# Normed feed-forward inputs, down products in groups of four, and an even split of the PSUM banks in a two-block transformer kernel

## The chip, the cores and the metric

The kernel runs on one core of a Trainium2 chip. The metric is the time of one execution on the device in microseconds (us): the median of the runs shown, and for the trace one execution that was profiled. PE is the matrix engine, DVE the vector engine, ACT the scalar engine, POOL the GpSimd engine, SP the engine that issues most transfers. SBUF holds the tiles (128 partitions), PSUM takes the results of the matrix engine in 8 banks of 512 fp32 columns.

## The reference

L = 1040 tokens (16 meta tokens and 1024 of the input), model width 1024, all in fp32. Two layers, then a second block:

```python
for layer in range(2):
    h = rms_norm(hs, norm_mix_pre[layer])
    mix = pool_mixer(h, ...) if layer == 0 else sliding_window_attention(h, k_blk, v_blk, ...)
    hs = hs + rms_norm(mix, norm_mix_post[layer])
    h = rms_norm(hs, norm_ffn_pre[layer])
    hs = hs + rms_norm(swiglu(h, w_gate_up[layer], w_down[layer]), norm_ffn_post[layer])
    if layer == 0:
        kv_in = rms_norm(hs, kv_norm)      # k, v of the attention of layer 1
x = hs[:, 16:]
h = x * (1 + scale) + shift                # scale, shift, gate from silu(c) @ w_ada
p = h @ w_in
out_a = gmlp_branch(p[..., :1536])         # u * (causal spatial product of LN(v)) * silu(gate)
out_b = rwkv7_branch(p[..., 1536:])        # token shift, decay, scan over time, LN, gate
x = layer_norm(ALPHA * x + gate * (concat(out_a, out_b) @ w_out), ln_g, ln_b)
```

The feed-forward width is 2816, 22 blocks of 128 (`NF`). A root-mean-square norm is a per-token factor times a per-channel gain, so it can be applied to the input of a product or to its result.

## The kernel before, in words

Activations lie with channels on partitions: 8 tiles (`KT`) of 128 channels by up to 512 or 528 tokens. The tokens go in two halves, A and B. In layer 0 half A is two chunks of 264 tokens and half B one of 512; in layer 1 each half is one chunk of 512. All large products are done as three reduced-precision fp32 products, high by high, low by high and high by low (`mm3`), for which each input is split into a high part (an ACT copy, `xh`, `hh`, `wh`) and a low part (a DVE subtraction, `xl`, `hl`, `wl`). Weights are loaded 512 KB at a time by SP into `wr` and split by `split_weight` (ACT L329, DVE L330); four split sets and two raw ones are in the pool.

The program is written by generator threads that a planner (`run`, L220) steps: it takes the ready thread of highest priority, and a thread may yield planned time, wait for an event, or acquire a resource. That sets the order of the matrix engine's instructions. The other engines' instructions are ordered by priorities that `soon` raises. `main` (priority 0) runs `mixer0`, then four feed-forward passes a0A, a0B (layer 0), a1A, a1B (layer 1), then the second block of half B; `attentions` (priority 1) runs beside a0B and a1A and then does the second block of half A beside a1B; `out_first`, the output product of half A with its layer norm `final`, is spawned at priority -1 (L1619).

A feed-forward pass (`ffn`): for each f of 22, `up(f)` makes the gate product `pg` and the up product `pu` (8 x 3 matmuls each). Their inputs are the unnormed activations times the gain g, so the evictions multiply by the token factor `sb` of the norm: DVE L599 (gate times sb), ACT L604 (tanh of half of it), DVE L605, DVE L606 (up times sb), DVE L607 (the product `fg`), ACT L610 (`hh`), DVE L611 (`hl`). In a0A it is L599, a Silu, L602, L607. After two f's, `down` makes for each of 8 row blocks one PSUM tile of 2 x 3 matmuls and adds it to `acc` in SBUF (DVE L627; the first group copies, ACT L625). The last two f's go through `last` (L644), which makes the parts of three row blocks that don't need f = 21 first, finishes chunk by chunk and starts `finish` for each. `finish` (L394) norms the result, adds the old residual (L424, L425), stores it, splits hn x g into xh and xl (L435, L439), sets the event `x` on which the next pass starts, and only then works out the factor (`st_n`, `sb_n`; event `s`, waited for once per pass at f = 0).

`mixer0` does half A of the first mixer and spawns `second_half` (L535), which after the first finish reads blocks 5 to 9 in one burst (`blocks(5, 10)`) and makes the bands two at a time. In `second` (L1377), once half A is through, `rwkv(p, h)` for p = 0 to 3 acquires 15 tiles (`T`) each; `out_first` acquires 28 and gives 12 of them back when its `final` is done. At the start of half B two lines raise all priorities to their absolute value, so `out_first` runs then at +1. PSUM: pool `psg` (products) has 3 banks, `pss` (attention scores, rwkv and small products) 5.

Of the kernel before, what the change touches and what calls it, by code (L numbers as in the profile page):

```python
# [183 lines left out]
class K:  # L184
# [124 lines left out]
    def split_weight(self, src, name, gain=None, halves=False):  # L309
# [12 lines left out]
        ld = nc.sync.dma_start(out=raw, in_=src)  # L322
# [71 lines left out]
    def finish(self, y, sq, ch, ci, g_post, g_pre, src, dst, X):  # L394
# [21 lines left out]
        mod = g_pre == "mod"  # L416
        sqn = None if mod else self.ht(f"sqn_{nm}")
        for k in range(KT):
            fetch(k + 3)
            hn = y[k][:, s]  # L420
            if X["h"][k] is None:
                X["h"][k], X["l"][k] = self.ht(f"xh_{nm}_{k}", F32R), self.ht(f"xl_{nm}_{k}", F32R)
            xh, xl = X["h"][k][:, s], X["l"][k][:, s]
# [3 lines left out]
            if mod:  # L427
                t = self.tt(f"md_{nm}_{k}")[:, :w]
                nc.scalar.activation(out=t, in_=hn, func=AF.Identity, scale=self.mod[:, 8 + k:9 + k], bias=self.mod[:, k:k + 1])
                nc.scalar.activation(out=xh, in_=t, func=AF.Copy)  # L430
                nc.vector.tensor_tensor(out=xl, in0=t, in1=xh.bitcast(F32), op=ALU.subtract)
            else:
                g = None if g_pre is None else self.v(g_pre, k)
                self.sq_add(sqn, hn, w, k == 0, self.eng(X["name"], 2, k))
                nc.scalar.activation(out=xh, in_=hn, func=AF.Copy, **({} if g is None else dict(scale=g)))  # L435
                if g is None:
                    nc.vector.tensor_tensor(out=xl, in0=hn, in1=xh.bitcast(F32), op=ALU.subtract)
# [5 lines left out]
        if not mod:  # L443
            yield w_nsum
            dg = self.stats_sum(sqn, ch, f"n{nm}")
            yield w_nspread
            X["s"][ci] = self.stats_spread(dg, ch, f"n{nm}")
# [3 lines left out]
    def mixer0(self, Xs):  # L451
# [83 lines left out]
        def second_half():  # L535
# [3 lines left out]
            blocks(5, 10)  # L539
            yield 15000  # L540
            ch, y, sq = H0[1][0], [], self.ht("sqy0_10")
            for i in range(2):
                sp = [band(ch, "10", 2 * i + k) for k in range(2)]
                yield 9000
# [23 lines left out]
    def ffn(self, layer, X, chunks, tail):  # L568
# [6 lines left out]
        def up(f):  # L575
# [12 lines left out]
            for ci, (c0, w, _) in enumerate(chunks):  # L588
# [4 lines left out]
                if f == 0:  # L593
                    yield ("ev", f"s{nm}_{ci}")
                sb = X["s"][ci][:, :w]
# [1074 lines left out]
```

## Time and profile before

| | us |
|---|---|
| median of 3 runs (2833.78 to 2845.5) | 2837.9 |
| the profiled execution | 2839.37 |
| its span on the core | 2837.6 |

| engine | busy, share of the span |
|---|---|
| PE | 2629.9 us, 93% |
| DVE | 1745.2 us, 62% |
| ACT | 1068.7 us, 38% |
| POOL | 348.2 us, 12% |

The mean granted clock of the matrix engine is 0.956 of full speed. A share of busy time is an average: a stage in which PE is busy throughout at full clock can only be shortened by less work, one in which it waits or runs at a lower clock by an earlier arrival of what it waits for.

### The profile page before, as it was taken

How to read it: one execution, taken by the hardware profiler on the slowest of the kernel's cores; microseconds unless marked ns; L12 is line 12 of the kernel's file. 1: busy time of each engine (PE TensorE's matmuls, PEld its weight loads, DVE VectorE, ACT ScalarE, POOL GpSimd, SP SyncE). 2: the span in 40 equal slices, each digit the busy share in tenths (PEclk: the TensorE clock that was granted, in tenths of full speed). 3: DMA queues.
4: the chain of work that ended last, by engine and by line, in shares of the span. 5: the costliest groups of instructions: out<-in, count | busy, mean ns of one | idle time of the engine just before them, and what ended most of it. 6: DMA issues, size and time to landing. Idle time of an engine off the chain costs nothing.

```text
span 2837.6 us, 41913 instructions
## 1 busy us (share of the span) xinstructions
PE 2629.9 (93%) x16381; PEld 2183.1 (77%) x16381; DVE 1745.2 (62%) x3366; ACT 1068.7 (38%) x1996; POOL 348.2 (12%) x324
## 2 busy tenths in 40 slices
PE   5878999989999999999999999999999999999966
PEld 4868999978877877787778777877777777777756
DVE  6446665575666476756664774527756557666744
ACT  5333222354444333545443344323322224443423
POOL 3111000120000021100000210001101002311213
PEclk8888999999999999999999999999998999999968
DMA  4264433333222243332223444433232225443322
GB/s 151 98 143 135 153 123 97 96 123 101 90 64 82 89 141 101 130 100 79 88 69 101 141 134 133 127 129 116 73 110 63 97 90 196 153 137 118 104 94 67
DMA packets 156885, 314.57 MB, mean 111 GB/s; under 512 B 44792, under 2 KB 68778, under 8 KB 156688
## 3 DMA queue, kind: packets, MB, share of 16 engines
q1 hardware_dynamic: 147792, 296.06, 32.4%
q10 hardware_dynamic: 8896, 15.84, 2.3%
q8 instruction: 129, 2.11, 0.3%
q14 instruction: 68, 0.56, 0.1%
HBM read 266.60 MB, written 45.23 MB: 110 GB/s over the span
## 4 chain that ended last, share of the span: by engine, by line
PE 72%; DVE 12%; issue 5%; DMA 4%; ACT 3%; POOL 3%; SPq 1%; DVEq 0%; POOLq 0%; ACTq 0%
PE po L265 6%; PE pda0A L265 5%; PE pua0A L265 4%; PE pga0A L265 4%; PE pda1A L265 4%; PE pua1A L265 4%; PE pda0B L265 4%; PE pga0B L265 4%; PE pua0B L265 3%; PE pga1A L265 3%; PE pq L265 3%; PE pga1B L265 3%; PE pua1B L265 3%; PE pda1B L265 2%; PE pv L265 2%
## 5 line engine op out<-in xcount | busy, mean ns | idle before, releaser
L265 PE MATMUL pua0A<-xh_a0A,wh_ua0A 128*128 128x264 f32 x352 | 106.2, 302 | 15.9 <-DVE fg L599 15.9
L265 PE MATMUL po<-oc,wh_wo 128*128 128x256 f32 (+1 forms) x384 | 94.4, 339 | 17.1 <-ACT oc L1403 15.2
L265 PE MATMUL pda0A<-hha0A,wh_da0A 128*128 128x264 f32 x352 | 105.0, 298 | 4.9 <-DVE acca0A L627 4.2
L265 PE MATMUL pga0A<-xh_a0A,wl_ga0A 128*128 128x264 f32 x352 | 102.1, 290 | 6.0 <-DVE wl_ga0A L330 6.0
L265 PE MATMUL pga0A<-xh_a0A,wh_ga0A 128*128 128x264 f32 x352 | 103.3, 294 | 2.6 <-ACT xh_a0A L435 2.6
L265 PE MATMUL pua0A<-xh_a0A,wl_ua0A 128*128 128x264 f32 x352 | 104.8, 298 | 0.0
L265 PE MATMUL pua0A<-xl_a0A,wh_ua0A 128*128 128x264 f32 x352 | 104.7, 297 | 0.0
L265 PE MATMUL pga0A<-xl_a0A,wh_ga0A 128*128 128x264 f32 x352 | 102.4, 291 | 0.5 <-DVE xl_a0A L439 0.5
L265 PE MATMUL pda0A<-hla0A,wh_da0A 128*128 128x264 f32 x352 | 102.0, 290 | 0.0
L265 PE MATMUL pda0A<-hha0A,wl_da0A 128*128 128x264 f32 x352 | 101.9, 289 | 0.0
L392 POOL TENSOR_TENSOR sqo<-sqo,sq 128x512 f32<-128x512 f32 x4 | 5.2, 1298 | 739.1 <-ACT sq L391 739.1
L810 ACT ACTIVATE l<-l,anm 128x256 f32<-128x256 f32 x128 | 63.5, 497 | 74.3 <-DVE anm L802 74.2
L265 PE MATMUL pda0B<-hha0B,wh_da0B 128*128 128x512 f32 x176 | 75.3, 428 | 15.2 <-DVE fg L599 10.8
L265 PEld LDWEIGHTS po<-oc,wh_wo 128*128 128x128 f32 x384 | 68.5, 203 | 25.5 <-ACT oc L1403 15.9
L265 PE MATMUL pda1A<-hha1A,wh_da1A 128*128 128x512 f32 x176 | 74.2, 422 | 13.7 <-DVE fg L599 7.8
L265 PEld LDWEIGHTS pua0A<-xh_a0A,wh_ua0A 128*128 128x128 f32 x352 | 71.2, 202 | 17.5 <-DVE fg L599 16.6
L265 PE MATMUL pda1B<-hha1B,wh_da1B 128*128 128x512 f32 x176 | 74.3, 422 | 10.6 <-DVE acca1B L627 5.7
L604 ACT ACTIVATE fu<-fg 128x512 f32<-128x512 f32 x66 | 41.5, 629 | 98.7 <-DVE fg L599 98.3
L627 DVE TENSOR_TENSOR acca0A<-pda0A,acca0A 128x264 f32<-128x264 f32 x160 | 64.9, 428 | 22.1 <-PE pda0A L265 21.3
L794 DVE CUSTOM_DVE_ANT_0 l<-qk,bias,sink 128x256 f32<-128x256 f32 x128 | 56.6, 479 | 32.3 <-PE qk L265 32.3
L265 PE MATMUL pua1A<-xh_a1A,wh_ua1A 128*128 128x512 f32 x176 | 71.4, 405 | 4.4 <-DVE fg L599 4.4
L265 PEld LDWEIGHTS pda0A<-hha0A,wh_da0A 128*128 128x128 f32 x352 | 68.3, 194 | 9.3 <-DVE acca0A L627 6.3
(798 smaller groups left out, 8546.9 us busy)
## 6 DMA issues: line engine op xcount, KB each, us to landing
ada<-in_w_ada_dram ACTq DMA_DIRECT2D x24, 512.0 KB, 4.1
wr_ga0A<-in_wgu_dram SPq DMA_DIRECT2D x22, 512.0 KB, 3.5
wr_ua0A<-in_wgu_dram SPq DMA_DIRECT2D x22, 512.0 KB, 4.0
wr_da0A<-in_wdn_dram SPq DMA_DIRECT2D x22, 512.0 KB, 3.8
wr_ga0B<-in_wgu_dram SPq DMA_DIRECT2D x22, 512.0 KB, 3.5
wr_ua0B<-in_wgu_dram SPq DMA_DIRECT2D x22, 512.0 KB, 3.5
wr_da0B<-in_wdn_dram SPq DMA_DIRECT2D x22, 512.0 KB, 3.5
wr_ga1A<-in_wgu_dram SPq DMA_DIRECT2D x22, 512.0 KB, 3.6
```

The source lines that it names most:

```text
L265: self.last = self.nc.tensor.matmul(out, lhsT, rhs, start=start, stop=stop).ins
L392: (eng or nc.gpsimd).tensor_tensor(out=acc[:, :w], in0=acc[:, :w], in1=sq[:, :w], op=ALU.add)
L604: nc.scalar.activation(out=u, in_=g, func=AF.Tanh, scale=0.5)
L627: nc.vector.tensor_tensor(out=o, in0=p[:, :ch[1]], in1=o, op=ALU.add)
L794: nc.vector.tensor_tensor_reduce(out=l[:, bb, e], in0=pq[e][:, 256 * bb:256 * bb + 256], in1=bias[:, e], scale=1.0, scalar=sink[:, 8 * e + ...
L810: nc.scalar.activation(out=lf[:, x], in_=lf[:, x], func=AF.Exp, bias=nm4[:, x:x + 1], accum_out=den[:, x:x + 1])
```

## The change

It has five parts. (1) `finish` of the inputs of a0B, a1A, a1B, of the attention's inputs b0, works out the second norm first and splits hn x g x sb (a new tile `nx`), so the event `x` comes after the factor, and evictions have no `sb`: tanh reads PSUM directly, and DVE has three instructions for an f instead of five. The attention's `scaled` is dropped likewise. a0A keeps the old form (`X["a0A"]["s"] = {}`). (2) `down` takes four f's at a time in a0A, a0B and a1A (groups of 4, 4, 4, 4, 4, 2) and two in a1B; a weight tile holds two column blocks of four f's (or four of two f's), so rows of a load are 1 KB or 2 KB instead of 4 KB, with the number of loads unchanged; a PSUM tile gets 12 matmuls instead of 6 and is added once; the products of a group come after the first `up` of the next. `last` goes. (3) The blocks and bands of `second_half` are spread by yields. (4) The two lines in `second` that raise the priorities go, so `out_first` stays at -1. (5) `psg` has 4 banks and `pss` 4.

```diff
@@ finish @@
+        late = not mod and "s" not in X
...
-                self.sq_add(sqn, hn, w, k == 0, self.eng(X["name"], 2, k))
-                nc.scalar.activation(out=xh, in_=hn, func=AF.Copy, **({} if g is None else dict(scale=g)))
...
+        yield w_nsum
+        dg = self.stats_sum(sqn, ch, f"n{nm}")
+        yield w_nspread
+        sb = self.stats_spread(dg, ch, f"n{nm}")
...
+        for k in range(KT):
...
+            t = self.tt(f"nx_{nm}_{k}")[:, :w]
+            if g_pre is None:
+                nc.vector.tensor_tensor(out=t, in0=hn, in1=sb[:, :w], op=ALU.mult)
+            else:
+                nc.vector.scalar_tensor_tensor(out=t, in0=hn, scalar=self.v(g_pre, k), in1=sb[:, :w], op0=ALU.mult, op1=ALU.mult)
+            nc.scalar.activation(out=xh, in_=t, func=AF.Copy)
+            nc.vector.tensor_tensor(out=xl, in0=t, in1=xh.bitcast(F32), op=ALU.subtract)
+            yield w_col * w * 0.5
+        yield w_x
         self.events.add(f"x{nm}")
@@ mixer0, second_half @@
-            blocks(5, 10)
-            yield 15000
+            for j in range(5, 10):
+                blocks(j, j + 1)
+                yield 6000
+            yield 9000
@@ ffn @@
+                else:
+                    with self.soon(PRIO):
+                        nc.scalar.activation(out=u, in_=pg[:, :w], func=AF.Tanh, scale=0.5)
+                        nc.vector.scalar_tensor_tensor(out=g, in0=u, scalar=1.0, in1=pg[:, :w], op0=ALU.add, op1=ALU.mult)
+                        nc.vector.scalar_tensor_tensor(out=g, in0=pu[:, :w], scalar=0.5, in1=g, op0=ALU.mult, op1=ALU.mult)
...
+            n = 8 // len(fs)
...
+                src = A["wdn"][layer, fs[0]:fs[-1] + 1, :, 128 * mp:128 * (mp + n)].rearrange("f p c -> p f c")
+                w = self.split_weight(src, f"d{nm}_{fs[0]}_{mp}")
...
+        for g0, g1 in zip(groups, groups[1:]):
+            yield from up(g1[0])
+            yield from down(g0)
+            for f in g1[1:]:
+                yield from up(f)
+        yield from down(groups[-1], True)
@@ second @@
             self.res["G"] = 5
-            for th in self.threads:
-                th[2] = abs(th[2])
@@ main @@
-        yield from self.ffn(1, X["a1B"], H1[1], ("g_fpost1", "mod", self.hsd[2], self.hsd[3], X["b1B"]))
+        yield from self.ffn(1, X["a1B"], H1[1], ("g_fpost1", "mod", self.hsd[2], self.hsd[3], X["b1B"]), 2)
@@ pools @@
-            self.ps = P("psg", 3, space=PSUM)
-            self.p2 = P("pss", 5, space=PSUM)
+            self.ps = P("psg", 4, space=PSUM)
+            self.p2 = P("pss", 4, space=PSUM)
```

The first place is PE in the second block of half B, where the scan of the last head group p = 3 begins (`zw3`; names carry p and the half, `pgg21` is a gate product of half B, `yo1` the transposed output of p = 1). Before, it begins while gate products are still to come:

```order
L265 MATMUL zw3_1_23334<-wd3_1_23238,wup3_1_23243 128x512
L265 MATMUL za3_1_23335<-wd3_1_23238,wup3_1_23243 128x512
L269 MATMUL kt3_1_23354<-eye_75,kq3_1_23245 128x128 x4
L265 MATMUL S1_1_0_23367<-HV0_1_1_22284,W00_1_1_22164 64x64
L265 MATMUL S1_1_0_23367<-HV0_1_1_22284,W10_1_1_22166 64x64
L265 MATMUL S1_1_0_23367<-S1_1_23365,QM0_1_1_23310 64x64 x2
L265 MATMUL P12_1_23373<-T2_1_22735,N2_1_22974 64x64 x16
L265 MATMUL pgg21_23404<-xh_b1B_0_0_20869,wh_gg21_23399 128x512
L265 MATMUL pgg21_23404<-xl_b1B_0_0_20870,wh_gg21_23399 128x512
L265 MATMUL pgg21_23404<-xh_b1B_0_0_20869,wl_gg21_23400 128x512
```

and now after the last of them, after the layer norm of half A (`st_ln0`, `sb_ln0`) and after `yo1`:

```order
L265 MATMUL gp1_1_23184<-wsp1_1_22689,gx1_1_22879 64x128 x8
L265 MATMUL st_ln0_23202<-ones_76,sql0_22903 128x1 x4
L269 MATMUL sb_ln0_23213<-eye_75,dg_ln0_23211 128x128 x4
L269 MATMUL yo1_1_23256<-eye_75,yt1_1_23148 128x128 x4
L265 MATMUL zw3_1_23276<-wd3_1_23247,wup3_1_23252 128x512
L265 MATMUL za3_1_23277<-wd3_1_23247,wup3_1_23252 128x512
L269 MATMUL kt3_1_23296<-eye_75,kq3_1_23254 128x128 x4
L265 MATMUL gc2_1_23307<-wsp2_1_23267,ones_76 64x128 x2
L269 MATMUL kn3_1_23316<-eye_75,kq3_1_23254 128x128 x4
L269 MATMUL gt2_1_23338<-eye_75,gv2_1_23314 128x128 x4
```

So `zw3` has moved behind all products of half B, and what ran beside its chain before has run already.

The second place is DVE late in pass a0B. Before, one f takes L599, L605, L606, L607 and L611, with weight splits (L330) between:

```order
L599 TENSOR_TENSOR fg_10122<-pga0B_19_0_10048,rb_na0B_0_2240 128x512
L605 SCALAR_TENSOR_TENSOR fg_10122<-fu_10123,fg_10122 128x512
L606 SCALAR_TENSOR_TENSOR fu_10123<-pua0B_19_0_10090,rb_na0B_0_2240 128x512
L607 TENSOR_TENSOR fg_10122<-fg_10122,fu_10123 128x512
L330 TENSOR_TENSOR wl_da0B_19_10214<-wr_da0B_19_10212,wh_da0B_19_10213 128x1024
L611 TENSOR_TENSOR hla0B_19_10130<-fg_10122,hha0B_19_10129 128x512
L599 TENSOR_TENSOR fg_10195<-pga0B_20_0_10139,rb_na0B_0_2240 128x512
L605 SCALAR_TENSOR_TENSOR fg_10195<-fu_10196,fg_10195 128x512
```

and now, at the last f of the pass, L632, L633 and L637, with the sums of the last group (L648) and the new splits of the inputs of pass a1A (`nx_a1A`, L463, and `xl_a1A`, L465) between:

```order
L632 SCALAR_TENSOR_TENSOR fg_10076<-fu_10077,pga0B_21_0_10001 128x512
L633 SCALAR_TENSOR_TENSOR fg_10076<-pua0B_21_0_10045,fg_10076 128x512
L637 TENSOR_TENSOR hla0B_21_10082<-fg_10076,hha0B_21_10081 128x512
L463 SCALAR_TENSOR_TENSOR nx_a1A_0_2_10100<-yo20_9369,vecs_74,rb_na1A_0_10031 128x512
L648 TENSOR_TENSOR acca0B_0_6110<-pda0B_20_0_0_10091,acca0B_0_6110 128x512
L330 TENSOR_TENSOR wl_ua1A_0_10270<-wr_ua1A_0_10268,wh_ua1A_0_10269 128x1024
L648 TENSOR_TENSOR acca0B_1_6125<-pda0B_20_1_0_10107,acca0B_1_6125 128x512
L465 TENSOR_TENSOR xl_a1A_0_2_10099<-nx_a1A_0_2_10100,xh_a1A_0_2_10098 128x512
L648 TENSOR_TENSOR acca0B_2_6166<-pda0B_20_2_0_10124,acca0B_2_6166 128x512
L463 SCALAR_TENSOR_TENSOR nx_a1A_0_3_10116<-yo30_9405,vecs_74,rb_na1A_0_10031 128x512
L648 TENSOR_TENSOR acca0B_3_6181<-pda0B_20_3_0_10141,acca0B_3_6181 128x512
L465 TENSOR_TENSOR xl_a1A_0_3_10115<-nx_a1A_0_3_10116,xh_a1A_0_3_10114 128x512
```

So two instructions of an f have gone, and the splits of the next pass's inputs have moved among the last sums of this one.

## Rows read from the trace of the kernel before

**Rows 1.** Windows by stage: stretch, length, busy us (instructions), PEclk, DMA share, GB/s.
```profile
0.00:65.60 65.60, 31.51 (x210) 30.09 (x211) 39.66 (x83) 34.88 (x77) 22.54 (x31) 0.88 0.46 153
65.60:264.00 198.40, 159.68 (x1057) 151.39 (x1056) 107.44 (x181) 70.09 (x129) 37.01 (x35) 0.84 0.47 128
264.00:558.30 294.30, 292.11 (x2323) 284.78 (x2322) 179.85 (x336) 80.19 (x128) 8.28 (x10) 0.99 0.37 118
558.30:1116.00 557.70, 538.25 (x2731) 432.27 (x2732) 359.64 (x709) 241.97 (x517) 52.13 (x43) 0.98 0.31 99
1116.00:1664.10 548.10, 529.78 (x2646) 426.32 (x2645) 356.04 (x674) 236.98 (x493) 45.21 (x29) 0.98 0.31 101
1664.10:2364.80 700.70, 671.19 (x4197) 526.26 (x4196) 413.54 (x765) 223.94 (x336) 67.88 (x71) 0.98 0.35 111
2364.80:2837.60 472.80, 407.38 (x3226) 331.98 (x3226) 289.07 (x622) 180.62 (x319) 115.15 (x106) 0.89 0.37 120
```

**Rows 2.** PE's waits, 65.6:264: line, releaser, total us, times, longest.
```profile
PE pua0A L265 <- DVE fg L599: 15.9, 3, 6.6
PE po L265 <- DVE fu L602: 7.4, 1, 7.4
```

**Rows 3.** PE's waits, 558.3:1116 (pass a0B).
```profile
PE pda0B L265 <- DVE fg L599: 10.8, 6, 3.3
PE pua0B L265 <- DVE fg L599: 3.2, 1, 3.2
```

**Rows 4.** PE's waits, 1116:1664.1 (pass a1A).
```profile
PE pda1A L265 <- DVE fg L599: 7.8, 4, 3.0
```

**Rows 5.** PE's waits, 1664.1:2364.8 (pass a1B).
```profile
PE pda1B L265 <- DVE acca1B L627: 5.7, 5, 1.7
```

**Rows 6.** Groups of instructions on DVE: busy us, mean ns, idle before.
```profile
L794 DVE CUSTOM_DVE_ANT_0 l<-qk,bias,sink 128x256 f32<-128x256 f32 x128 | 56.6, 479 | 32.3 <-PE qk L265 32.3
...
L627 DVE TENSOR_TENSOR acca0B<-pda0B,acca0B 128x512 f32<-128x512 f32 x80 | 54.6, 686 | 12.9 <-PE pda0B L265 12.4
...
L605 DVE SCALAR_TENSOR_TENSOR fg<-fu,fg 128x512 f32<-128x512 f32 x66 | 47.5, 719 | 15.8 <-ACT fu L604 15.6
...
L330 DVE TENSOR_TENSOR wl_da0B<-wr_da0B,wh_da0B 128x1024 fp32r<-128x1024 f32 x22 | 27.7, 1258 | 7.8 <-ACT wh_da0B L329 7.5
```

**Rows 7.** Groups of instructions on ACT.
```profile
L604 ACT ACTIVATE fu<-fg 128x512 f32<-128x512 f32 x66 | 41.5, 629 | 98.7 <-DVE fg L599 98.3
```

**Rows 8.** Timeline of PE, 512-column products: start us, duration us.
```profile
2499.70 0.39 PE L265 MATMUL pr<-xl_b1B,wh_r 128*128 128x512 f32 x1
2499.93 0.40 PE L265 MATMUL pr<-xh_b1B,wl_r 128*128 128x512 f32 x1
```

**Rows 9.** Timeline of DVE in the start-up, with the idle time before.
```profile
179.11 1.28 DVE L922 SCALAR_TENSOR_TENSOR moda<-ada,silu_c,moda 128x1024 f32<-128x1024 f32 x1 [10.78 <-DMA ada<-in_w_ada_dram]
```

**Rows 10.** Window of ten us in the start-up, columns as in Rows 1.
```profile
160.00:170.00 10.00, 4.98 (x35) 4.76 (x34) 2.23 (x3) 2.06 (x3) 0.00 (x0) 0.79 0.95 197
```

**Rows 11.** DMA issues: count, KB each, median us to landing.
```profile
wr_da0B<-in_wdn_dram SPq DMA_DIRECT2D x22, 512.0 KB, 3.5
...
bias<-reld SPq DMA_DIRECT2D x16, 256.0 KB, 2.8
```

**Rows 12.** Timeline of PE, first zw of p=3, second half.
```profile
2626.84 0.69 PE L265 MATMUL zw<-wd,wup 64*128 64x512 f32 x1
```

**Rows 13.** Groups on PE in 2610:2678.
```profile
L265 PE MATMUL A<-AR,BK 64*128 64x128 f32 x32 | 3.4, 285 | 0.0
```

**Rows 14.** Timeline of PE in the tail.
```profile
2678.27 0.60 PE L269 MATMUL yo<-eye,yt 128*128 128x128 f32 x4
...
2711.13 1.97 PE L265 MATMUL gp<-wsp,gx 128*64 128x128 f32 x16 [5.56 <-POOL gx L1046]
...
2752.30 1.31 PE L265 MATMUL po<-oc,wh_wo 128*128 128x256 f32 x2 [6.30 <-ACT oc L1403]
...
2760.94 0.60 PE L269 MATMUL yo<-eye,yt 128*128 128x128 f32 x4
```

More of the change, by code (lines that the diff above doesn't have):

```diff
@@ L420, in finish @@
             hn = y[k][:, s]
-            if X["h"][k] is None:
+            if not late and X["h"][k] is None:
                 X["h"][k], X["l"][k] = self.ht(f"xh_{nm}_{k}", F32R), self.ht(f"xl_{nm}_{k}", F32R)
-            xh, xl = X["h"][k][:, s], X["l"][k][:, s]
             nc.vector.scalar_tensor_tensor(out=hn, in0=hn, scalar=self.v(g_post, k), in1=rb[:, :w], op0=ALU.mult, op1=ALU.mult)
@@ L565, in mixer0, with ffn @@
         self.spawn(second_half())
[L568 removed]
+    def ffn(self, layer, X, chunks, tail, size=4):
         nc, A = self.nc, self.A
@@ L628, in add @@
             return o
-        def down(fs):
-            first = fs[0] == 0
-            yield ("acq", "ring", 1)
-            dw = down_weights(fs)
-            for m in range(KT):
-                for ci, ch in enumerate(chunks):
-                    p = self.pg(f"pd{nm}_{fs[0]}_{m}_{ci}")
-                    yield from self.mm3(p, units(dw, fs, m, ch), ch[1])
-                    if acc[m] is None:
-                        acc[m] = self.ht(f"acc{nm}_{m}")
-                    add(m, ch, p, first)
-            self.done(len(fs))
-            self.res["ring"] += 1
@@ L667, in ffn, with down @@
-        yield from up(0)
-        for f in range(1, NF - 2, 2):
-            yield from up(f)
-            yield from up(f + 1)
-            yield from down([f - 1, f])
-        yield from up(NF - 1)
-        yield from last([NF - 2, NF - 1])
+        def down(fs, end=False):
+            n = 8 // len(fs)
+            sq = {}
+            for mp in range(0, KT, n):
+                yield ("acq", "ring", 1)
+                src = A["wdn"][layer, fs[0]:fs[-1] + 1, :, 128 * mp:128 * (mp + n)].rearrange("f p c -> p f c")
+                w = self.split_weight(src, f"d{nm}_{fs[0]}_{mp}")
+                for m in range(mp, mp + n):
+                    for ci, ch in enumerate(chunks):
+                        c = slice(ch[0] - base, ch[0] - base + ch[1])
+                        p = self.pg(f"pd{nm}_{fs[0]}_{m}_{ci}")
+                        yield from self.mm3(p, [(w, 128 * (n * i + m - mp), hid[f][0][:, c], hid[f][1][:, c]) for i, f in enumerate(fs)], ch[1])
+                        o = add(m, ch, p, fs[0] == 0)
+                        if end:
+                            if m == 0:
+                                sq[ci] = self.ht(f"sqf{nm}_{ci}")
+                            with self.soon(PRIO):
+                                self.sq_add(sq[ci], o, ch[1], m == 0, self.eng(tail[-1]["name"], 0, m))
+                self.done()
+                self.res["ring"] += 1
+            if end:
+                for ci, ch in enumerate(chunks):
+                    self.spawn(self.finish(acc, sq[ci], ch, ci, *tail))
@@ L676, in attention @@
+        f = 0
+        groups = []
+        while f < NF:
+            groups.append(list(range(f, min(f + size, NF))))
+            f += size
+        for f in groups[0]:
+            yield from up(f)
+        for g0, g1 in zip(groups, groups[1:]):
[4 more added lines that the diff above has]
+        yield from down(groups[-1], True)
     def attention(self, h, X, Xn):
@@ L737, in attention @@
             qf[i] = self.ht(f"qf{i}{h}")
-            scaled(qf[i], p, q0, nq)
+            nc.scalar.activation(out=qf[i][:, :nq], in_=p[:, :nq], func=AF.Identity, bias=self.v("b_q", i))
         blocks = [vT0] if h == 0 else []
```

109 lines of the change are left out of this document (43 added, 66 removed).

## The prediction

> **What bounds the kernel now.** I read the windows by stage first, then the matrix engine's waits in each stage, then the groups of instructions on the engines that it waits for, and last the timeline of the tail. The windows [rows 1] are to be read by subtraction: a stretch's length less PE's busy time is idle time, and one less the granted clock, times the length, is about what slow matmuls cost. From 264 to 558.3 us PE is busy 292.1 of 294.3 us at a clock of 0.99: nothing but less work could shorten it, and the change removes no matmul. The pass a0B (558.3 to 1116) loses 19.5 us of idle time and 0.02 x 558 = 11 us of clock, a1A 18.3 and 11, a1B with the second block of half A beside it 29.5 and 14. The start (65.6 to 264) loses 38.7 us idle and 0.16 x 198 = 32 us of clock, the tail 65 and 52. So of 2837.6 us some 170 are waits in the stages that the change touches and 120 are clock, and most of both lie at the two ends, not in the feed-forward passes on which the change does most.
>
> Within the passes PE mostly waits for the eviction of a gate product: 10.8 and 3.2 us in a0B [rows 3], 7.8 in a1A [rows 4]. In a1B the largest row is the sum of the down products, 5.7 us [rows 5]. DVE is busy 359.6 of 557.7 us in a0B [rows 1]: not a bound by its sum, but its instructions come in bursts, and a burst is what these waits are.
>
> **The evictions and sums of a0B and a1A.** For each of 22 f's two DVE instructions of 512 columns go. DVE's rows give 0.72 us for the gate step and 0.69 for a sum [rows 6], so about 1.4 us, 31 us of DVE for a pass. The down sums halve, from 80 to 40 of 0.69 us [rows 6]: 27 us more. The new splits cost 16 instructions of about 0.7 us ahead of a pass, 11 us, of which 8 (the low parts) were there before. Together DVE falls from 360 to about 305 us in a pass. None of that is a gain by itself, since PE is the busy engine; the gain is at most the idle and the clock loss, 30 us in a0B and 29 in a1A. The chain that PE waits for gets shorter by L599 (the tanh of 0.63 us [rows 7] now reads PSUM), a fourth product bank lets PE run one product further ahead, and a down tile lasts 12 matmuls of 0.23 us [rows 8] = 2.8 us instead of 1.4, four times the 0.69 us of its sum. I take two thirds, since the attention products that run beside these passes wait for DVE too: **-20** (bounds -30, all of it, and -8, the gate waits alone after half of them move) for a0B and **-19** (-29 to -8) for a1A. a1B keeps groups of two and the sums as they are, and waits mostly for those; of its 29.5 us about 14 belong to the feed-forward, I take half: **-7** (-14 to 0).
>
> **The bank that is taken away.** `pss` goes from 5 to 4. The attention fills two banks with scores for a set of heads; each is read by two DVE instructions of 0.48 us [rows 6], and DVE stood idle 32.3 us for these scores over 128 of them [rows 6], so DVE waits for PE there and not PE for DVE. If in each of the 32 sets the fourth bank came late by both readers, it would be 32 x 0.96 = 31 us; if the feed-forward products always fill in, nothing. I take a quarter, **+8** (0 to 31), since products of the feed-forward stand ready to fill in, but not at every set. In a1B the scan of half A shares that pool: **+4** (0 to 12), by the same share.
>
> **Ends of passes.** Before, `last` put nine matmuls of three tiles (9 x 0.23 = 2.1 us) under the chain of the last f (0.72 + 0.63 + 0.69, about 2.0 us [rows 6, 7]); now only the three matmuls of the earlier f of one tile, 0.7 us. I take 1.3 us for each of four passes, **+5** (0 to 8). The late splits cost more: a1A starts only when nx, the copy and xl are through. DVE then has 8 sums (5.5 us), 16 split instructions (11.3) and four weight splits of 1.26 us (5.0) [rows 6], 22 us. PE has the last group of two f's, 8 tiles of 6 matmuls = 11.1 us, and one product of 24 matmuls, 5.5 us [rows 8]: 17. So 5 us are open, of which attention products fill some; **+3** each at a1A and a1B, **+6** (4 to 17).
>
> **The start-up.** PE waits there 15.9 us in three long waits for the gate's eviction and 7.4 for the up product's [rows 2]. The evictions are not slow: DVE stands for 10.78 us behind a modulation weight that had not landed [rows 9], in a stretch in which the DMA engines are busy 0.95 of the time and PE runs 5 of 10 us at a clock of 0.79 [rows 10]. The change leaves the weights of the modulation and the large bias write where they are, but spreads the burst of block reads and takes a splitting step of the a0B inputs away from the first finish. I take **-15** of the 71 us that the stretch loses (bounds -50, the long waits and most of the clock go; +15, the spread reads run later into the same crowd).
>
> **Weight rows of 1 KB.** A down load of 512 KB lands in 3.5 us with 4 KB rows; the bias reads, 256 KB in 1 KB rows, land in 2.8 [rows 11]. Whether the rows' length or the transfer's fixed part makes the second number, the row does not tell; by it a load of 512 KB in 1 KB rows takes between 3.5 and 5.6 us. A tile of such weights feeds two column blocks of 12 matmuls, 24 x 0.23 = 5.5 us of PE [rows 8], and split sets stand ahead of it, so this is hidden: **0** (0 to 10, a first load or two of each pass uncovered).
>
> Small transfers, under 2 KB, carry overhead and should be batched to 4 or 8 KB: so the Trainium skill, "Perfetto Trace Analysis", section DMA Optimizations; it speaks against this change. The trace bears it out in part (half the bytes take four fifths of the time [rows 11]). By the row the sum keeps its 0; by the rule, if landing times double, it gets the +120 of case (e) below.
>
> **The tail.** The two lines that go keep `out_first` and its `final` at the lowest priority, and 12 tiles come free only when `final` is done, so the scan of p = 3 starts late. Before, its first product stands at 2626.84 [rows 12], its last (the transposed output) at 2760.94 [rows 14]. Now `zw3` follows `yo1`, which stood at 2678.27 [rows 14] behind the last large product. Ahead of `yo1` then goes what p = 2 and 3 did there, some 18 us of matmuls (ten for p = 3, of which A with 3.4 is the largest of nine groups [rows 13], and eight for p = 2), and 9 of the earlier norm; in come some 18 us of waits that those products covered. So `zw3` starts near 2669, 42 us later. Its chain was 134 us long; in it stood about 8 us of large products that are now through, 10.5 us of waiting of which 5.56 are POOL's `gp` [rows 14], and some 12 us behind p = 2: I take 30 off and 5 on for the interleaving with p = 2, which now runs at the same time. That leaves 109 us, and its end at about 2778; 17 us after 2760.94. Nothing of it is given back, because the output products wait for that chain already (6.30 [rows 14]), and what runs uncovered at a lower clock adds 3: **+20** (0, if the scan's chain loses as much as its start; +50, if it loses nothing).
>
> **The sum.** -20 - 19 - 7 - 15 + 8 + 4 + 5 + 6 + 20 = -18. The profiled execution took 2839.37 us, 1.5 above the median of 2837.9, so 2839.4 - 18 = 2821 by the profile and 2820 beside the median.
>
> **The rivals.**
> (a) The start-up falls into place: with the burst spread, the weights land in time, PE's long waits go and its clock stays up, -50 instead of -15: **2785**. For it: DMA at 0.95 in exactly the waiting stretch [rows 10]. Against: the bias write of the same stretch stays.
> (b) The start-up gives nothing, the attention's bank costs what the evictions save in part: -18 + 15 = -3, **2836**, no change. For it: what DVE waits for there is a weight of the modulation [rows 9], which isn't touched. Against: the blocks and bands of the second half run in that very stretch.
> (c) Slower: the tail. If p = 3's chain keeps its 134 us when it starts at 2669, and p = 2 beside it adds 10, it is 144 instead of 109 and the tail costs 55 instead of 20: -18 + 35, **2856**. The sum is above nothing from a chain of 127 us on, above 0.5% from 141. For it: p = 3 and p = 2 share DVE, ACT and POOL and run on top of each other; 65 of 473 us are idle there already [rows 1].
> (d) The eviction waits only change their place: the products wait less and the attention's scores, with a bank fewer, more. Half of the gain in a0B and a1A goes (+20), the bank costs half of its bound (+8), the late splits 5 more, and the start-up gives nothing (+15): -18 + 48 = +30, **2869**. For it: both kernels fill all 8 banks. Against: DVE has 55 us less to do in each pass.
> (e) The loads in 1 KB rows land in a little over twice the 3.5 us, 7.5: 2 us over the 5.5 of a tile, 60 such tiles in the three passes, +120: **2940**. Against: the DMA share is 0.31 in a0B and a1A [rows 1].
>
> **How the numbers follow.** Forecast 0.40 (own range 2795 to 2830); (a) 0.18; (b) 0.18; (c) 0.14; (d) 0.07; (e) 0.03. The predicted time is 2820. The range reaches from (a) with most of the evictions' bound besides (another -19), 2766, to between (c) and (d), 2864; it leaves out (e), most of (d), the far end of (a) and some of (c), under 2 in 10. A measurement of this kernel tells about 0.5%, 14 us, from no change: faster (below 2823.7) holds (a) and four fifths of the forecast, 0.50; same holds (b) and the last fifth, 0.26; slower (over 2852) holds (c), (d) and (e), 0.24.
>
> **What would show it.** In the profile of the changed kernel: a0B and a1A shorter by about 20 us each with DVE near 305 us in them; gate waits under 5 us in each; down tiles of 12 matmuls 2.8 us apart; the wait at the start of a1A under 6 us; in the start-up still one wait of over 5 us; `zw` of p = 3 behind the last gate product, and its output some 15 to 20 us later against that stretch's start. The prediction is wrong if a0B and a1A do not get shorter, if PE waits for down weights there, or if the stretch after the last feed-forward pass grows by more than 40 us or not at all.

## The result, and the profile after

The changed kernel takes 2801.4 us (median of 4 runs, 2798.96 to 2803.73) beside 2839.5 for the kernel before (4 runs, one more than in the first table), a ratio of 0.9865, 95% interval 0.9842 to 0.9889: 38 us faster, where 18 were forecast. The profiled execution took 2798.96 us, its span is 2797.2.

These are the windows by stage of the changed kernel, cut at the same places as [rows 1] (columns as there, without the start; a0A is one row here; before, its two rows add to 492.7 us):

```profile
65.80:521.70 455.90, 436.67 (x3370) 424.10 (x3370) 260.49 (x442) 151.32 (x257) 44.65 (x43) 0.96 0.45 132
521.70:1051.70 530.00, 528.04 (x2739) 428.63 (x2738) 305.14 (x625) 240.10 (x518) 47.35 (x43) 1.00 0.33 104
1051.70:1586.10 534.40, 525.99 (x2646) 425.38 (x2645) 303.71 (x595) 238.93 (x501) 47.56 (x31) 0.99 0.32 103
1586.10:2275.00 688.90, 667.52 (x4197) 523.38 (x4195) 392.18 (x729) 223.79 (x342) 70.04 (x72) 0.99 0.35 112
2275.00:2797.20 522.20, 422.86 (x3226) 341.27 (x3226) 283.50 (x622) 178.14 (x316) 115.27 (x107) 0.85 0.35 110
```

Read the lengths against [rows 1]: a0A 492.7 to 455.9 (-36.8), a0B 557.7 to 530.0 (-27.7), a1A 548.1 to 534.4 (-13.7), a1B 700.7 to 688.9 (-11.8), and the tail 472.8 to 522.2 (+49.4). Four stages give 90 us and the last takes back 49. In a0B PE is now busy 528.0 of 530.0 us at a clock of 1.00: there is almost nothing left to win there without less work. In the tail PE is busy for 422.9 us in place of 407.4 with the same number of instructions, while the clock fell from 0.89 to 0.85, and its idle time grew from 65 to 99 us.

PE's waits in a0B (line, what it waited for, total us, times, longest), all that the trace lists; those for the gate's eviction [rows 3] are gone:

```profile
PE pda0B L265 <- ACT hha0B L636: 1.1, 1, 1.1
PE pv L265 <- DVE am L801: 0.7, 1, 0.7
PE pda0B L265 <- DVE hla0B L637: 0.2, 1, 0.2
```

In a1A, the two largest are at its start, for the new splits, and the 7.8 us of [rows 4] are gone:

```profile
PE pga1A L265 <- ACT xh_a1A L464: 2.2, 2, 1.6
PE pga1A L265 <- DVE xl_a1A L465: 1.6, 1, 1.6
```

DVE's groups (columns as in [rows 6]) show the evictions as predicted, 0.68 us for the gate step, 40 sums instead of 80; and DVE's idle time for the attention's scores fell from 32.3 to 9.4 us, with a bank fewer for them:

```profile
L801 DVE CUSTOM_DVE_ANT_0 l<-qk,bias,sink 128x256 f32<-128x256 f32 x128 | 55.4, 480 | 9.4 <-PE qk L265 9.4
...
L648 DVE TENSOR_TENSOR acca0B<-pda0B,acca0B 128x512 f32<-128x512 f32 x40 | 27.4, 688 | 22.4 <-PE pda0B L265 22.3
...
L632 DVE SCALAR_TENSOR_TENSOR fg<-fu,pga0B 128x512 f32<-128x512 f32 x22 | 15.0, 683 | 6.8 <-ACT fu L631 6.6
```

In the tail, the timeline of PE: `yo` of p = 1, the first `zw` of p = 3, and `yo` of p = 3:

```profile
2592.56 1.06 PE L269 MATMUL yo<-eye,yt 128*128 128x128 f32 x4
2593.55 1.22 PE L265 MATMUL zw<-wd,wup 64*128 64x512 f32 x1
...
2722.33 1.08 PE L269 MATMUL yo<-eye,yt 128*128 128x128 f32 x4 [5.83 <-DVE yt L1368]
```

The window between the last large product (2541) and that `zw`:

```profile
2541.00:2594.00 53.00, 30.64 (x250) 23.57 (x250) 26.69 (x63) 15.62 (x32) 25.13 (x22) 0.67 0.17 55
```

`zw` of p = 3 stands 318.6 us after the stage's start, where it stood 262 before [rows 12], and PE works through the 53 us ahead of it at a clock of 0.67 and 58% busy. From there to the last `yo` it takes 128.8 us, where it took 134.1 [rows 12, 14].

### The profile page after: what moved, and what is told of

Its sections match the earlier page's. It is cut to its first block, busy times and chain, and to the rows that moved or that the text cites. A ratio compares the mean times of both kernels' runs of the same rounds, so it can differ in the third digit from the quotient of the medians.

```text
span 2797.2 us, 41641 instructions
## 1 busy us (share of the span) xinstructions
PE 2612.4 (93%) x16381; PEld 2172.6 (78%) x16381; DVE 1585.8 (57%) x3092; ACT 1067.2 (38%) x2009; POOL 347.0 (12%) x324
## 5 line engine op out<-in xcount | busy, mean ns | idle before, releaser
L265 PE MATMUL pga1A<-xh_a1A,wh_ga1A 128*128 128x512 f32 x176 | 70.9, 403 | 2.2 <-ACT xh_a1A L464 2.2
L265 PE MATMUL pua1B<-xh_a1B,wh_ua1B 128*128 128x512 f32 x176 | 72.2, 410 | 0.0
L265 PE MATMUL pga1B<-xh_a1B,wh_ga1B 128*128 128x512 f32 x176 | 71.3, 405 | 0.8 <-ACT xh_a1B L464 0.6
L265 PE MATMUL pga1B<-xl_a1B,wh_ga1B 128*128 128x512 f32 x176 | 70.4, 400 | 1.7 <-DVE xl_a1B L465 1.7
L265 PEld LDWEIGHTS pga0A<-xh_a0A,wh_ga0A 128*128 128x128 f32 x352 | 67.8, 193 | 5.2 <-ACT xh_a0A L438 3.0
L265 PE MATMUL pga1A<-xl_a1A,wh_ga1A 128*128 128x512 f32 x176 | 70.0, 398 | 1.6 <-DVE xl_a1A L465 1.6
```

The source lines that it names most:

```text
L265: self.last = self.nc.tensor.matmul(out, lhsT, rhs, start=start, stop=stop).ins
```

## The experiments

All times are medians; experiments 1 to 4, 5 to 8 and 9 to 12 each ran on one chip with their own runs of the kernel before (2839.7, 2835.1 and 2837.5 us), so ratios are compared. "Changed kernel" is the kernel with the whole change. A stage's length comes from one profiled execution, and "longer" and "shorter" are against the windows of the kernel that the experiment starts from.

**1. The raised priorities put back into the changed kernel.**

```diff
             self.res["G"] = 5
+            for th in self.threads:
+                th[2] = abs(th[2])
```

> The changed kernel with the two lines back that raise the priorities at the start of half B. If the 50 us that the last stretch grew (472.8 to 522.7 us) come from the late scan of p = 3 alone, the last stretch goes back to about 475 us and the kernel takes 2755 (2745 to 2765). If they come from the bank taken from pss, or from a stretch that simply inherits what the passes ahead did earlier, the last stretch stays above 505 and the kernel takes 2785 to 2805.

2752.9 us, ratio 0.9700 (0.9687 to 0.9713). The window of its last stage, and from its timeline `zw` and the last `yo` of p = 3:

```profile
2275.00:2749.00 474.00, 407.85 (x3226) 330.46 (x3226) 290.15 (x622) 180.59 (x319) 113.89 (x107) 0.90 0.37 121
```

```profile
2538.83 0.69 PE L265 MATMUL zw<-wd,wup 64*128 64x512 f32 x1
...
2672.15 0.60 PE L269 MATMUL yo<-eye,yt 128*128 128x128 f32 x4
```

The other stages agree with the changed kernel's within 0.2 us. The tail is back at 474.0, at a clock of 0.90, and `zw` at 263.8 us into the stage. Taking out these two lines, with the late scan that follows from it, cost 48 us. What is left against the 472.8 us of before is 1 us, so a bank fewer in `pss` costs this stage next to nothing.

**2. The two lines taken out of the kernel before**, and nothing else.

> The kernel before without the two lines that raise the priorities, nothing else changed. Late scan alone: the last stretch grows by 40 to 50 us and the time goes to about 2885. If the growth needs the other parts of the change (4 banks for pss), the time stays at 2840 to 2855, which also holds if the prediction's +20 was right and the other 30 us of the last stretch came from elsewhere.

2883.4 us, ratio 1.0160 (1.0138 to 1.0183). Its last stage:

```profile
2361.90:2880.80 518.90, 426.82 (x3226) 344.66 (x3226) 282.04 (x623) 178.75 (x317) 119.53 (x106) 0.84 0.34 109
```

46 us longer than before, at a clock of 0.84. The effect needs no other part of the change; experiments 1 and 2 agree. Up to the end of a1B this run has the same instructions in the same order on PE, DVE, ACT and POOL as the kernel before, and yet its passes take 489.2, 554.7, 547.4 and 705.5 us where the kernel before took 492.7, 557.7, 548.1 and 700.7. So differences of up to about 5 us between windows of two executions on the side of the kernel before show nothing.

**3. Only the spread block reads and bands, in the kernel before.**

```diff
-            blocks(5, 10)
-            yield 15000
+            for j in range(5, 10):
+                blocks(j, j + 1)
+                yield 6000
+            yield 9000
```

(and the bands one at a time)

> The kernel before with only the block reads and bands of the first mixer's second half spread. If the spread is what took 37 us from the pass a0A, it goes from 492.7 to 460 and the kernel to about 2805. If a0A gained by the down groups of four and the fourth product bank, the time stays within 8 us of 2839. My term of the prediction, -15 for the spread and the first finish, lies between.

2830.8 us, ratio 0.9968 (0.9956 to 0.9981). The window of a0A, and the largest of its waits:

```profile
65.30:546.80 481.50, 441.97 (x3377) 426.75 (x3376) 286.81 (x517) 149.98 (x257) 46.69 (x44) 0.95 0.41 125
```

```profile
PE pua0A L265 <- DVE fg L603: 27.3, 3, 19.7
```

-11.2 us in a0A (8.8 on the median), within neither clean case. PE still waits 27.3 us for gate evictions, 19.7 of it at once: the wait moved and the rest of the stage ran better.

**4. The burst put back into the changed kernel**, the edit of experiment 3 reversed.

> The changed kernel with the burst of block reads and the bands two at a time, as before. Spread as cause: a0A goes back to about 485 us and the kernel to 2830. Groups and bank as cause: a0A stays below 465 and the kernel within 8 us of 2801.

2825.8 us, ratio 0.9953 (0.9940 to 0.9965). a0A, and its largest wait:

```profile
65.40:546.20 480.80, 437.78 (x3371) 425.11 (x3369) 263.20 (x442) 150.74 (x257) 48.70 (x43) 0.95 0.42 125
```

```profile
PE pua0A L265 <- DVE wl_ua0A L330: 23.9, 1, 23.9
```

+24.9 us in a0A, of which 23.9 are one wait for the split of an up weight. So the spread is worth 11 us in the old kernel and 25 in the new: with the other parts in place it is what keeps PE from one long stall. What held that split up is in DVE's timeline: two instructions ahead of it, DVE stood 33.94 us for a weight of the modulation (the number in brackets; the split follows at 177.66). With the spread, in the changed kernel, DVE still stands 26.28 us for such a weight, longer than the 10.78 of before [rows 9], but PE waits for nothing longer than 6.8 us in this pass:

```profile
175.85 1.29 DVE L925 SCALAR_TENSOR_TENSOR moda<-ada,silu_c,moda 128x1024 f32<-128x1024 f32 x1 [33.94 <-DMA ada<-in_w_ada_dram]
```

```profile
170.88 1.28 DVE L929 SCALAR_TENSOR_TENSOR moda<-ada,silu_c,moda 128x1024 f32<-128x1024 f32 x1 [26.28 <-DMA ada<-in_w_ada_dram]
```

The first line is this run's, the second the changed kernel's. So the change did not end DVE's stop, but PE got through it: from 140 to 180 us it is busy 33.2 us in the changed kernel and 16.1 with the burst. What gives it that work is not shown.

**5. The changed kernel with 3 banks for `psg` and 5 for `pss`.**

```diff
-            self.ps = P("psg", 4, space=PSUM)
-            self.p2 = P("pss", 4, space=PSUM)
+            self.ps = P("psg", 3, space=PSUM)
+            self.p2 = P("pss", 5, space=PSUM)
```

> The changed kernel with 3 banks for psg and 5 for pss, as before. If the shorter evictions and fewer sums made a0B and a1A shorter, the two passes stay within 8 us together of 530.0 and 534.4 and the kernel stays at 2795 to 2812. If the fourth product bank did it, they go back by over 25 us together, gate waits return, and the kernel takes 2825 or more. If the bank cost the attention what I put (8 us), the passes get a little shorter.

2814.0 us, ratio 0.9922 (0.9909 to 0.9936). Its passes a0A to a1B:

```profile
65.20:529.20 464.00, 439.41 (x3371) 425.51 (x3369) 260.70 (x444) 151.26 (x257) 45.59 (x44) 0.96 0.43 129
529.20:1061.90 532.70, 528.67 (x2737) 427.78 (x2738) 302.79 (x623) 239.79 (x518) 47.84 (x42) 1.00 0.31 103
1061.90:1596.70 534.80, 526.10 (x2646) 423.92 (x2645) 303.26 (x595) 238.66 (x501) 45.91 (x31) 0.99 0.31 103
1596.70:2291.40 694.70, 668.27 (x4197) 520.99 (x4195) 392.70 (x729) 224.18 (x341) 69.29 (x72) 0.99 0.34 111
```

a0A +8.1, a0B +2.7, a1A +0.4, a1B +5.8. In a0B and a1A, where the bank was to matter, it hardly does.

**6. The kernel before with 4 banks for each pool**, the same edit the other way round.

> The kernel before with 4 banks for each pool, nothing else. Bank as cause: a0B and a1A shorter by 25 us or more together (from 557.7 and 548.1), the kernel at 2812 or less. Evictions and sums as cause: within 8 us of 2839. Bank missed by the attention (the rival of waits that change their place): 2845 to 2870, with waits for scores in the passes.

2803.4 us, ratio 0.9890 (0.9876 to 0.9904): 32 us alone, nearly as much as the 38 of the whole change. Its passes:

```profile
65.20:550.60 485.40, 445.37 (x3377) 431.46 (x3377) 285.53 (x517) 149.81 (x257) 44.45 (x44) 0.94 0.41 124
550.60:1096.20 545.60, 532.39 (x2734) 428.14 (x2733) 359.23 (x709) 241.50 (x517) 51.82 (x43) 0.99 0.30 101
1096.20:1633.70 537.50, 524.37 (x2645) 422.09 (x2644) 355.13 (x674) 236.95 (x493) 44.87 (x29) 1.00 0.31 103
1633.70:2326.70 693.00, 668.06 (x4197) 524.09 (x4195) 413.90 (x765) 222.83 (x336) 67.28 (x71) 0.98 0.34 112
```

a0A -7.3, a0B -12.1, a1A -10.6, a1B -7.7. Two of its waits in a0B:

```profile
PE pda0B L265 <- DVE fg L599: 4.7, 4, 1.9
...
PE pv L265 <- DVE am L794: 1.4, 2, 0.7
```

The gate waits fell from 10.8 to 4.7 us and the 3.2 of the up product [rows 3] are gone; the attention waits 1.4 us for its scores in a0B and, by the same listing, 4.4 us in a1A, where no such wait was listed before. Two numbers that seem to contradict each other (12 us of a0B with it, 2.7 without it) say that the bank and some other part remove the same waits. The next runs look for it.

**7. The changed kernel with down groups of two in all passes** (weight rows of 2 KB).

```diff
-    def ffn(self, layer, X, chunks, tail, size=4):
+    def ffn(self, layer, X, chunks, tail, size=2):
```

> The changed kernel with down groups of two in all passes (loads in 2 KB rows). If the halved sums are half of the gain of a0B and a1A, these passes get longer by 10 to 15 us each; if the shorter evictions alone did it, by under 4. In a0A the waits for the weights' splits tell: with pairs, 88 sums of 264 columns more; if the groups of four are what took the 25 us beside the spread, a0A goes from 455.9 to 480. If loads in 1 KB rows had cost anything, a pass would get shorter.

2820.2 us, ratio 0.9948 (0.9936 to 0.9961). a0A and a0B:

```profile
66.50:537.20 470.70, 438.51 (x3371) 424.82 (x3371) 288.75 (x522) 151.01 (x257) 44.02 (x43) 0.96 0.43 128
537.20:1073.60 536.40, 530.61 (x2739) 427.94 (x2738) 333.33 (x671) 244.40 (x524) 50.21 (x45) 1.00 0.31 103
```

a0A +14.8, a0B +6.4, a1A 2.5 shorter, and 6 longer in the tail, which the change of this run doesn't touch and which I leave unexplained. The 10 to 15 us each that I expected for a0B and a1A did not come. Only a1A got shorter with rows of 2 KB, and there PE no longer waits the 3.8 us for the new splits at its start; so this does not show that rows of 1 KB cost anything.

**8. The factor back in the evictions of the changed kernel's a0B, a1A and a1B.** The tanh then follows a product with `sb`, as before, and the event `x` comes ahead of the factor.

```diff
-        X["a0A"]["s"] = {}
+        for n in ("a0A", "a0B", "a1A", "a1B"):
+            X[n]["s"] = {}
...
-                        nc.scalar.activation(out=g, in_=g, func=AF.Silu)
-                        nc.vector.tensor_tensor(out=u, in0=pu[:, :w], in1=sb, op=ALU.mult)
+                        if nm == "a0A":
+                            nc.scalar.activation(out=g, in_=g, func=AF.Silu)
+                            nc.vector.tensor_tensor(out=u, in0=pu[:, :w], in1=sb, op=ALU.mult)
+                        else:
+                            nc.scalar.activation(out=u, in_=g, func=AF.Tanh, scale=0.5)
+                            nc.vector.scalar_tensor_tensor(out=g, in0=u, scalar=1.0, in1=g, op0=ALU.add, op1=ALU.mult)
+                            nc.vector.scalar_tensor_tensor(out=u, in0=pu[:, :w], scalar=0.5, in1=sb, op0=ALU.mult, op1=ALU.mult)
```

> The changed kernel with the factor of the norm put back into the evictions of a0B, a1A and a1B (five instructions of DVE for an f, inputs split before the factor is known); the attention's inputs stay normed ahead. Evictions as cause: a0B and a1A longer by 10 to 20 us each, DVE back up by about 31 us in each, gate waits back. Sums and bank as cause: under 5 us each; the starts of a1A and a1B, where PE now waits 3.8 and 2.3 us for the new splits, get shorter by these.

2808.2 us, ratio 0.9902 (0.9887 to 0.9917). a0B, a1A, a1B:

```profile
526.20:1061.40 535.20, 530.64 (x2739) 430.02 (x2738) 334.78 (x668) 244.73 (x524) 52.97 (x45) 0.99 0.31 103
1061.40:1590.40 529.00, 523.69 (x2645) 424.51 (x2644) 329.53 (x633) 240.80 (x501) 45.46 (x29) 0.99 0.31 104
1590.40:2285.80 695.40, 667.77 (x4197) 524.42 (x4195) 412.61 (x764) 222.53 (x335) 67.55 (x71) 0.98 0.34 112
```

a0B +5.2, a1B +6.5, and a1A 5.4 us shorter. DVE did go up (305 to 335 us in a0B), but the waits didn't return: two DVE instructions an f are not what PE waited for once the groups and the bank are there. Whether a1A's 5.4 us are a gain or were only moved out of a0B, experiment 11 tells.

**9. Of the change only the groups of four**, in a kernel that is otherwise as before (burst, 3 and 5 banks, factor in the evictions, raised priorities). It is the changed kernel with the edits of experiments 1, 4, 5 and 8; the attention's inputs stay normed ahead, as its new code needs, and `last` is gone, and a1B has the pairs of the new down code.

> The kernel before with, of the change, only the down groups of four (and the attention's inputs normed ahead, which comes with the new attention code): burst reads, 3 and 5 banks, the factor in the evictions, the raised priorities. If the bank and the groups each remove the same waits, this alone makes a0B and a1A shorter by 8 to 14 us each, as the bank alone did (12.1 and 10.6), and the kernel takes 2795 to 2815. If the groups only work with the bank, a0B and a1A stay within 4 us of 557.7 and 548.1. In a0A it should give 8 to 15 us.

2795.3 us, ratio 0.9849 (0.9836 to 0.9861): alone as much as the whole change, and in a0B and a1A more than the 8 to 14 us that I expected. Its passes:

```profile
65.80:548.10 482.30, 439.36 (x3371) 426.70 (x3369) 262.54 (x436) 150.77 (x257) 47.29 (x44) 0.95 0.42 125
548.10:1084.70 536.60, 529.32 (x2738) 427.79 (x2739) 334.10 (x665) 244.91 (x524) 51.76 (x44) 1.00 0.31 103
1084.70:1614.20 529.50, 524.41 (x2646) 423.82 (x2645) 330.02 (x634) 240.77 (x501) 45.10 (x29) 0.99 0.31 104
1614.20:2320.80 706.60, 673.39 (x4197) 527.43 (x4195) 413.58 (x764) 222.58 (x335) 67.19 (x71) 0.98 0.34 110
```

a0A -10.4, a0B -21.1, a1A -18.6, a1B (pairs here too) 5.9 longer. In a1A this is better than all parts together; a0B and a1A as one give 39.7 us, where all parts give 41.4.

**10. Of the change only the inputs normed ahead**, with the pairs of the new down code: the changed kernel with the edits of experiments 1, 4, 5 and 7.

> The kernel before with, of the change, only the inputs normed ahead of their split in a0B, a1A and a1B (and the pairs of the new down code, without the products that stood ahead at a pass's end): burst reads, 3 and 5 banks, raised priorities. If shorter evictions are a third way to the same waits: a0B and a1A shorter by 6 to 12 us each, kernel 2805 to 2822. If the late splits eat it up: within 8 us of 2839.

2816.8 us, ratio 0.9924 (0.9913 to 0.9936). a0B and a1A:

```profile
553.20:1095.10 541.90, 532.20 (x2737) 428.52 (x2738) 332.82 (x669) 244.44 (x524) 49.59 (x44) 1.00 0.31 102
1095.10:1640.90 545.80, 527.90 (x2645) 424.36 (x2644) 321.57 (x628) 237.23 (x496) 43.80 (x29) 0.99 0.31 101
```

a0B 15.8 and a1A 2.3 us shorter, a1B 3.5, a0A 4.4: a third way to the same waits in a0B; the other three are within the 5 us by which unchanged passes differ (2). That the late splits eat up the gain of a1A is not shown: at its start PE waits for no split in this run, and the waits listed in the pass are for the sums of pairs (8.2 us in six) and the copy `hha1A` (4.2). Experiments 9 and 10 share the attention's new inputs, the new down code and the loss of `last`; no run has these alone, so how much of their 21.1 and 15.8 us in a0B comes from what they share stays open.

**11. Experiment 1 with a1A as in experiment 8**, the name a1A alone added to a0A's.

> The changed kernel with the raised priorities, and a1A back to splitting its inputs before the factor is known (its evictions take the factor). Leaving the factor in the evictions made a1A 5.4 us shorter and a0B and a1B longer; if that holds for a1A alone, the pass takes 529 instead of 534 and the kernel 2747, 4 to 8 us under the 2752.9 with the raised priorities. If a1A only seemed shorter because a0B ended later, no difference.

2748.2 us, ratio 0.9682 (0.9670 to 0.9695); the interval overlaps that of experiment 1, so on the total it is not told apart. Its a1A:

```profile
1053.80:1584.10 530.30, 523.80 (x2646) 424.45 (x2645) 327.76 (x634) 238.23 (x497) 44.86 (x29) 0.99 0.31 104
```

530.3 for 534.3 us, as in experiments 8 and 9. But a0B, whose evictions this run leaves alone, takes 533.2 us for the 530.1 of experiment 1: the two passes together gain 0.9 us. So most of a1A's gain only moved across the border of the passes, and of experiment 8's +5.2 in a0B some 3 us may be of that kind.

**12. Experiment 1 with groups of four in a1B.**

```diff
-        yield from self.ffn(1, X["a1B"], H1[1], ("g_fpost1", "mod", self.hsd[2], self.hsd[3], X["b1B"]), 2)
+        yield from self.ffn(1, X["a1B"], H1[1], ("g_fpost1", "mod", self.hsd[2], self.hsd[3], X["b1B"]))
```

> The changed kernel with the raised priorities and down groups of four in a1B as well. PE is idle there for 20.9 of 688.9 us, of which the feed-forward's rows are under 8: at most 8 us shorter, 2745 to 2753. If four inputs held longer keep tiles from the scan of half A, the pass gets longer and the kernel takes over 2760.

2742.3 us, ratio 0.9665 (0.9652 to 0.9677), the fastest of all: 3.4% under the kernel before. Its a1B:

```profile
1586.10:2264.50 678.40, 663.77 (x4197) 521.36 (x4195) 368.31 (x689) 223.94 (x342) 72.87 (x72) 0.99 0.35 113
```

10.4 us shorter than in experiment 1, more than the 8 that I put as the most. 11 and 12 together were not tried.

What each part gives alone, in the kernel before, and costs when it is taken out of the changed one, in us by the windows (in a1B the changed kernel has pairs, so the row of the groups shows there only the new down code and chance; groups of four in a1B are experiment 12):

| part | a0A alone / taken out | a0B | a1A | a1B |
|---|---|---|---|---|
| spread | -11.2 / +24.9 | +1.5 / -0.8 | +0.6 / -0.7 | +0.3 / +3.3 |
| bank | -7.3 / +8.1 | -12.1 / +2.7 | -10.6 / +0.4 | -7.7 / +5.8 |
| groups of four | -10.4 / +14.8 | -21.1 / +6.4 | -18.6 / -2.5 | +5.9 / -1.1 |
| normed ahead | -4.4 / +4.3 | -15.8 / +5.2 | -2.3 / -5.4 | -3.5 / +6.5 |
| all together | -36.8 | -27.7 | -13.7 | -11.8 |

In a0B the three parts alone would add to 49 us, and the pass has 30 to give: they substitute for each other. In a0A the four add to 33 of the 37 when put in alone and to 52 when taken out one by one: there the spread and the groups are worth more with the others in place.

## Why the prediction was right, and where not

The sign was right and the time within the range, but that is in part luck: the four passes gave 90 us where 38 were forecast for them, the tail took 49 where 20 were, and these two errors point against each other. By the prediction's own list it is wrong in the tail, which grew by more than 40 us; DVE near 305 us, the gate waits, the wait at the start of a1A and one start-up wait of over 5 us came as listed.

**Evictions and sums of a0B and a1A** (-20, -19): 27.7 and 13.7, net of the bank's and the ends' terms below. DVE came to 305.1 and 303.7 us, as worked out, and what bounded the gain, the idle and clock loss of the pass, bounded it: a0B took nearly all of its 30. The cause was given too narrowly: groups of four alone remove 21 and 19 us (experiment 9), the bank alone 12 and 11 (6); the shorter evictions, which I named first, 16 and 2 (10; the parts that 9 and 10 share are not separated). a1B (-7) gave 11.8; the bank alone gives 7.7 there (6).

**The bank that is taken away** (+8, +4) had the wrong sign. The bound of 31 us priced only what the attention loses and put the gain of the fourth product bank into another term without a number. Alone it is worth 38 us over the four passes by the windows, 32 on the median, and the attention waits 5.8 us for its scores in a0B and a1A (6). A gap that keeps repeating on the engine that should be busy can mean that SBUF or PSUM has no room for the next tile: so the Trainium skill, "Perfetto Trace Analysis", section Optimization Strategy. The runs agree: with the pool of products grown from 3 banks to 4 the repeated gate waits of a0B fell from 10.8 to 4.7 us, though the number of banks in all stayed 8.

**Ends of passes** (+5, +6). At a1A PE waits 3.8 us for the late splits, where I put 3; with early splits the pass is 4 to 5 us shorter (8, 11), but a0B takes back 3 of the 4 (11), so their net cost is about 1 us. With pairs and the same late splits PE waits for none at a1A (7, 10). At a1B the same rows come to about 2.3 us. The term of the missing cover was not measured by itself.

**The start-up** (-15): a0A gave 36.8. The size of the spread was right, 11 us alone, but it was taken for the only part that acts there: groups and bank alone give 10.4 and 7.3 us (the 4.4 of the norm is within the 5 us by which unchanged passes differ). That DVE has 80 sums of 264 columns fewer there, and PE more to work on while a weight is late, would explain it; no run shows it by itself. Of the two rivals, (b) was right that DVE goes on standing for a weight of the modulation (26.28 us, experiment 4), and wrong that the start-up then gives nothing. The largest waits of a0A now are these, 6.8 us in one and 3.7:

```profile
PE pda0A L265 <- ACT acca0A L646: 6.8, 1, 6.8
...
PE pda0A L265 <- DVE fg L625: 3.7, 1, 3.7
```

**Weight rows of 1 KB** (0): right. From issue to landing, with rows of 1 KB, to be held against the 3.5 us of [rows 11] (in a1B, with rows of 2 KB, it is 4.0):

```profile
wr_da0A<-in_wdn_dram SPq DMA_DIRECT2D x22, 512.0 KB, 3.7
...
wr_da1A<-in_wdn_dram SPq DMA_DIRECT2D x22, 512.0 KB, 3.5
```

Small transfers, under 2 KB, have a significant overhead each: so the Trainium skill, "Perfetto Trace Analysis", section DMA Optimizations. Taken for the rows of a load, as the prediction took it, the rule does not show here: 512 KB in rows of 1 KB land in 3.5 to 3.7 us, as in rows of 4 KB, at a DMA share of 0.32 to 0.45.

**The tail** (+20, bounds 0 to 50): +49.4, at the edge. Two numbers were off. `zw` of p = 3 comes 56 us later in the stage, not 42: the matmuls ahead of it run without cover, at a clock of 0.67, and wait in turn for an ACT step of a scan (7.7 us) and for DVE steps of the norm and the scans (4.2, 3.9 and 3.4). And the chain, which I cut from 134 to 109 us by taking away products and waits, took 128.8. These are its windows before and after, from `zw` to the end of the last `yo`:

```profile
2626.84:2761.50 134.66, 105.00 (x1154) 84.46 (x1153) 77.41 (x180) 43.00 (x83) 25.56 (x22) 0.80 0.31 100
```

```profile
2593.55:2723.40 129.85, 82.35 (x920) 64.89 (x919) 70.27 (x182) 34.80 (x71) 19.19 (x17) 0.67 0.28 84
```

23 us of matmul time left the chain and it got 5 us shorter: PE's idle time in it rose from 29.7 to 47.5 us, and the clock fell from 0.80 to 0.67. So most of what I took out was filler, and the end moved by 51 of the 56 us; how much of the kept length is the lower clock and how much are the chain's own steps, no run separates. In experiment 2 the chain takes 128 us as well. That is rival (c)'s mechanism (a chain that keeps its length, 55 us), which I gave 0.14; with the other terms as forecast (-38) it would have ended at +11, no faster than before; what kept the sign is that the passes gave 90 us and not 38 net. The last `yo` of p = 3 stands 447.3 us into the stage, 51 later than before, not 15 to 20. Experiments 1 and 2 show its size from both sides, 48 and 46 us.

## What to carry to other kernels

Before several remedies for the same wait are priced one after the other, bound them by the idle and clock loss of the stage, and give that bound once: in a0B each of three parts, as far as they could be put in alone, took 40 to 70% of it, and together they took it once. Compare neighbouring passes as one where a part moves work across their border. When a chain of small steps is moved behind the large products, price it at its full length and at the clock that PE has without cover, not at its length less the filler that stood in it. A gain and a loss in different stages can be separated by undoing the losing line alone: it turned 1.4% into 3.0%.

## What the runs showed of the hardware that was not expected

At the start of a1A two DVE instructions take 1.75 us that take 0.7 elsewhere (`xl_a1A`, L465, shown here, and `nx_a1A`, L463, right behind it). The timeline of DVE, with the same instruction a little earlier:

```profile
1054.58 0.69 DVE L465 TENSOR_TENSOR xl_a1A<-nx_a1A,xh_a1A 128x512 fp32r<-128x512 f32 x1 [0.70 <-ACT xh_a1A L464]
...
1056.99 1.75 DVE L465 TENSOR_TENSOR xl_a1A<-nx_a1A,xh_a1A 128x512 fp32r<-128x512 f32 x1
```

and that of POOL beside it:

```profile
1056.17 3.71 POOL L392 TENSOR_TENSOR sqfa0B<-sqfa0B,sq 128x512 f32<-128x512 f32 x2 [3.63 <-ACT sq L391]
```

POOL's two additions run from 1056.17 to 1059.88, and the two DVE instructions that start in that time are the slow ones; the pass's start waits for these very splits. The weight split just before them, begun at 1055.85 ahead of the additions, took its usual 1.22 us. The whole trace shows the same: L424, a scaling step of the norm that also reads SBUF alone, has a median of 0.74 us in the 20 cases of 512 columns that are clear of POOL and of 1.78 in the 10 that lie almost wholly beside it, while the sums L648, which read PSUM, take 0.69 and 0.68. GpSimd and DVE share a read port of SBUF: so the Trainium skill, "Perfetto Trace Analysis", section Optimizing Scalar/DVE Operations. That fits these rows; no run here moved the additions away to test it.
